# A fused two-layer encoder on one core: the decay product of the first GLA head is put directly behind the output gate's products, with its columns, and the PSUM banks are taken in another turn

## The chip, the cores and the metric

The kernel runs on one core of one Trainium2 chip. The core has a matrix engine (TensorE; PE in the profile, PEld for its weight loads), a vector engine (VectorE, DVE), a scalar engine (ScalarE, ACT), GpSimd (POOL) and a queue that issues transfers (SyncE, SP). Matrix products land in PSUM, of which this kernel uses eight banks of 128 partitions x 512 float32. The metric is device time in microseconds (us), the median of several executions. Before the change it is 2389.67 us (three executions, 2388.23 to 2390.68).

## What is computed

Two layers over a sequence of 1024 frames of width 1024: forgetting attention, a dense SwiGLU, gated linear attention (GLA), and again a SwiGLU, each normed, shifted, scaled and gated by a conditioning vector. The change lies in the GLA mixer:

```python
proj = h @ w_in
q, k, v, r, a_lr = jnp.split(proj, [...], axis=-1)
log_alpha = jax.nn.log_sigmoid((a_lr @ w_a2 + b_a)) / GLA_TAU
b = jnp.cumsum(log_alpha.reshape(B, N, CHUNK, GLA_HEADS, GLA_HK), axis=2)
q_in = q * jnp.exp(b)
k_in = k * jnp.exp(-b)
A = jnp.where(tril, jnp.einsum('bnthk,bnshk->bnhts', q_in, k_in), 0.0)
o_intra = jnp.einsum('bnhts,bnshv->bnthv', A, v)
k_dec = k * jnp.exp(b_last[:, :, None] - b)
kv = jnp.einsum('bnshk,bnshv->bnhkv', k_dec, v)
o = o_intra + o_inter            # o_inter = q_in times the state carried from chunk to chunk
o = rms_normed(o) * g_o * jax.nn.silu(r)
```

There are four heads, with 128 key columns and 256 value columns each. `a_lr` is 16 columns wide, and `(a_lr @ w_a2 + b_a)` is the decay.

## The kernel before

Every float32 matrix is held as a high and a low part, and a product is made as three (`mm3`, lines 289 to 292: high by high, high by low, low by high). A projection of 512 frames of one head (`proj`) runs over 8 slices of the width, so it is 24 products of 128x512 into one bank. Values go the other way round (`proj_tok`): 24 products for 128 frames.

The GLA part works head by head. Names below are those of the profile, with the lines of the kernel before.

- `gv`: values of the first head, eight tiles of 128 frames (`gv_first`). The weights of the values carry the 16 gate columns along, so a tile is 272 wide, and ScalarE copies these 16 columns to `aS`.
- `gr`: the output gate r, in halves of 512 frames (`r_proj`); ScalarE takes `silu` of a bank into `gs_s` (line 2061).
- `aps` and `aT`: four 128x16 blocks of gate columns are transposed into one bank (`a_body`) and split into high and low parts by ScalarE (line 1874), VectorE (1875) and ScalarE (1876).
- `z`: the decay product, one matrix product for 512 frames (`gate_z`). ScalarE takes the absolute value of it (`t_s`, line 1910), VectorE a clipped copy (`b_s`, line 1911).
- `gate_body`: exponential and logarithm on ScalarE (1918, 1919), a difference on VectorE (1920), two running sums (1923, TENSOR_TENSOR_SCAN), small columns `dec` (1927 to 1929), then exponentials on ScalarE into `ei_s` and `t_s` (1933, 1934).
- `gk`: keys, in two halves (`head_front`). VectorE reads a bank twice, times `ei_s` into `gy_s` and times `t_s` (1948, 1949); then the high and low parts `kih`, `kil`.
- `gqp`: queries, in two halves, read twice (1963) and split into `gq00`, `gq01`.
- `head_back`: transposes of the decayed keys (`kdt`, `kdh`, `kdl`), scores (`at`), masked (`atz`, line 1985) and split into `ahl`, states (`kv`, `Sf`, `S_t`) and outputs (`go`); the second half of the gate's columns (dv 1) is woven between these.

Beside it, VectorE works off steps of the second layer's conditioning vector (`ad_s`, lines 488 and 490), each of which waits for small transfers from the `ada_w` matrix, and the weights of what comes next are loaded and split: high part by ScalarE (line 227), low part by GpSimd in three pieces and VectorE in one (line 231).

What sets the order: each engine works through its own queue in order. The queues are made ahead of time by a scheduler that takes instructions as the program writes them and moves them by its own estimate of when each is ready; `tc.issue_after(x)` keeps what is written under it behind `x` on x's engine. PSUM banks are handed out in turn by rings. `pj` has banks b0, b1, b2, and its turns are, in the order of the program: `gr` first half, `z` first half, `gr` second half, `z` second half, `gk`, `gk`, `gqp`, `gqp`. The ring of the first head's values (`gvr`) has b0, b1, b2, b5, b6. So before the change the second half of `gr` has b2, which the last tile of values has just used, and the second `gk` has b2 as well; the second `gqp` has b1, the bank of the first `gk`.

## Time and profile before

| what | value |
|---|---|
| time of the runs, median | 2389.67 us |
| the profiled execution's own time | 2393.87 us |
| its span | 2392.2 us |
| TensorE busy | 2362.3 us, 99% of the span |
| VectorE busy | 1770.5 us, 74% |
| ScalarE busy | 1128.8 us, 47% |
| GpSimd busy | 1046.5 us, 44% |
| mean granted clock of TensorE | 0.991 |

A row of a timeline has the start in us from the span's start, the duration in us, the engine, the kernel's line, the operation, output <- inputs, the shape, how many instructions are merged, and in brackets how long the engine stood idle before it and what ended that. A row of the waits view has who waited for whom, the us in total, how many times, and the longest. Matrix products overlap in the pipeline: a 128x512 one lasts 0.39 us in these rows and the next starts about 0.23 us after it. Idle time of VectorE, ScalarE or GpSimd costs nothing as long as TensorE does not wait for them.

### The profile page before, as it was taken

The numbers are of one execution on the slowest core, as the hardware profiler recorded it, in microseconds if no ns is written. First come the engines' busy times: TensorE is split into PE (matmuls) and PEld (weight loads), VectorE is DVE, ScalarE is ACT, GpSimd is POOL, SyncE is SP. The second block draws the span as 40 slices with busy tenths as digits, with TensorE's granted clock in tenths as the row PEclk, the third lists the DMA queues.
The fourth block names the chain that finished last, engine by engine and source line by source line (L and its number), as shares of the span: only waits on it lengthen the run. The fifth ranks groups of instructions, "written<-read, shape, count | busy, mean of one in ns | idle before, by whom it ended". The sixth has DMA issues, their size and how long they took to land.

```text
span 2392.2 us, 35827 instructions
## 1 busy us (share of the span) xinstructions
PE 2362.3 (99%) x12312; PEld 2012.5 (84%) x12312; DVE 1770.5 (74%) x2985; ACT 1128.8 (47%) x2178; POOL 1046.5 (44%) x976
## 2 busy tenths in 40 slices
PE   8999999999999999999999999999999999999998
PEld 6988888888888888888888798898888888888888
DVE  6577787886698788875798566655687877765787
ACT  6656565675443333345325555453443333345326
POOL 1334444533445566643264321212345666643262
PEclk8999999999999999999999999999999999999999
DMA  8423333342435545457655233334424544457664
GB/s 259 142 80 113 104 119 93 119 133 89 150 109 174 178 165 168 166 203 258 228 188 166 82 105 90 99 112 132 150 91 154 179 148 161 154 180 255 230 205 147
DMA packets 336366, 363.47 MB, mean 152 GB/s; under 512 B 24924, under 2 KB 278008, under 8 KB 336184
## 3 DMA queue, kind: packets, MB, share of 16 engines
q1 hardware_dynamic: 336184, 361.18, 46.3%
q8 instruction: 97, 1.59, 0.3%
q14 instruction: 85, 0.70, 0.1%
HBM read 268.22 MB, written 92.86 MB: 151 GB/s over the span
## 4 chain that ended last, share of the span: by engine, by line
PE 82%; DVE 8%; DMA 4%; ACT 2%; issue 2%; POOL 1%; SPq 1%; DVEq 0%; POOLq 0%; ACTq 0%
PE p_b L290 15%; PE p_b L292 15%; PE p_b L291 15%; PE o_b L1224 2%; PE t_b L1210 2%; PE qk_b L290 1%; PE qk_b L291 1%; PE qk_b L292 1%; PE gr_b L290 1%; PE gr_b L291 1%; PE vps_b L292 1%; PE vps_b L290 1%; PE vps_b L291 1%; PE gr_b L292 1%; PE s_b L1178 1%
## 5 line engine op out<-in xcount | busy, mean ns | idle before, releaser
L175 DVE TENSOR_TENSOR o_s<-xv_s,o_s 128x512 fp32r<-128x512 f32 (+1 forms) x376 | 326.7, 874 | 67.7 <-ACT o_s L174 67.3
L174 ACT CAST o_s<-xv_s 128x512 fp32r<-128x512 f32 (+1 forms) x376 | 216.4, 587 | 304.3 <-PE p_b L292 244.5
L291 PE MATMUL p_b<-B,o_s 128*128 128x512 f32 x608 | 237.8, 391 | 0.0
L292 PE MATMUL p_b<-B,o_s 128*128 128x512 f32 x608 | 237.2, 391 | 0.0
L290 PE MATMUL p_b<-B,o_s 128*128 128x512 f32 x608 | 236.0, 391 | 0.0
L889 POOL TENSOR_TENSOR ex_s<-xv_s,xv_s 128x512 f32<-128x512 f32 (+1 forms) x64 | 88.5, 1382 | 286.7 <-DMA xv_s<-in_ffn_w_in_dram 113.6
L1190 POOL TENSOR_SCALAR lp_s<-lp_s,st 128x128 f32<-128x128 f32 (+7 forms) x128 | 97.9, 769 | 249.5 <-DVE st L1189 235.5
L290 PE MATMUL p_b<-T,o_s 128*128 128x512 f32 x480 | 186.7, 389 | 0.0
L291 PE MATMUL p_b<-T,o_s 128*128 128x512 f32 x480 | 186.7, 389 | 0.0
L292 PE MATMUL p_b<-T,o_s 128*128 128x512 f32 x480 | 181.2, 389 | 0.0
L292 PEld LDWEIGHTS p_b<-B,o_s 128*128 128x128 f32 x608 | 114.7, 189 | 24.0
L290 PEld LDWEIGHTS p_b<-B,o_s 128*128 128x128 f32 x608 | 114.7, 189 | 23.9
L291 PEld LDWEIGHTS p_b<-B,o_s 128*128 128x128 f32 x608 | 114.7, 189 | 23.7
L1188 ACT ACTIVATE lp_s<-lp_s,st 128x128 f32<-128x128 f32 (+7 forms) x128 | 99.3, 776 | 62.3 <-DVE st L1184 61.2
L891 POOL TENSOR_TENSOR xv_s<-ex_s,xv_s 128x512 f32<-128x512 f32 (+1 forms) x64 | 87.3, 1365 | 63.1 <-DVE o_s L175 60.8
L174 ACT CAST pt_s<-t_b 128x512 fp32r<-128x512 f32 (+1 forms) x160 | 79.8, 547 | 71.9 <-PE t_b L1210 71.3
L231 POOL TENSOR_TENSOR w_l_s<-w__s,w_h_s 128x256 fp32r<-128x256 f32 x90 | 69.6, 802 | 94.2 <-ACT w_h_s L227 61.8
L175 DVE TENSOR_TENSOR pt_s<-t_b,pt_s 128x512 fp32r<-128x512 f32 (+1 forms) x160 | 96.3, 630 | 15.9 <-ACT pt_s L174 15.4
L1572 DVE TENSOR_TENSOR ex_s<-ex_s,p_b 128x512 f32<-128x512 f32 x140 | 93.6, 681 | 18.6 <-PE p_b L292 18.5
L290 PEld LDWEIGHTS p_b<-T,o_s 128*128 128x128 f32 x480 | 90.1, 188 | 18.8
L291 PEld LDWEIGHTS p_b<-T,o_s 128*128 128x128 f32 x480 | 90.1, 188 | 18.7
L292 PEld LDWEIGHTS p_b<-T,o_s 128*128 128x128 f32 x480 | 90.1, 188 | 18.6
(1967 smaller groups left out, 7408.3 us busy)
## 6 DMA issues: line engine op xcount, KB each, us to landing
xv_s<-in_ffn_w_in_dram SPq DMA_DIRECT2D x176, 256.0 KB, 3.3
hid_B<-x SPq DMA_DIRECT2D x70, 512.0 KB, 2.8
ad_s<-in_ada_w_dram SPq DMA_DIRECT2D x384, 64.0 KB, 2.4
hid_T<-x SPq DMA_DIRECT2D x36, 512.0 KB, 2.8
xv_s<-in_ffn_w_out_dram SPq DMA_DIRECT2D x96, 192.0 KB, 5.1
ada_s<-in_ada_w_dram SPq DMA_DIRECT2D x96, 128.0 KB, 2.8
xv_s<-in_ffn_w_out_dram SPq DMA_DIRECT2D x40, 256.0 KB, 2.8
T2o<-hid_T SPq DMA_DIRECT2D x18, 512.0 KB, 9.7
```

The lines of the kernel that those rows point to most:

```text
L174: nc.scalar.copy(hi, src)
L175: nc.vector.tensor_sub(lo, src, hi.bitcast(F32))
L231: (nc.gpsimd if i < 3 else nc.vector).tensor_sub(lo[:, cs], rw[:, cs], hi[:, cs].bitcast(F32))
L290: nc.tensor.matmul(ps, ah, bh, start=start, stop=False)
L291: nc.tensor.matmul(ps, ah, bl, start=False, stop=False)
L292: nc.tensor.matmul(ps, al, bh, start=False, stop=stop)
L889: nc.gpsimd.tensor_add(s1, a21, a22)
L891: nc.gpsimd.tensor_sub(a11, s1, a11)
L1188: nc.scalar.activation(lp, lp, AF.Exp, bias=mcur, scale=-1.0, accum_out=st[:, qi, 2:3])
L1190: nc.gpsimd.tensor_scalar(lp, lp, st[:, qi, 3:4], 1.0, op0=ALU.mult, op1=ALU.mult)
L1210: nc.tensor.transpose(tp[:, i, :], lps[qi][:, psl(2 * b + jj)], ident)
L1572: nc.vector.tensor_add(d, d if src is None else dest(G, src), ps)
```

## The change

Four things are written differently, all for the first head.

1. After the ring of the values has been made, the turn of `pj` is moved on by one bank: `gr` takes b1 and b0, `z` b2 and b1, `gk` b2 and b0, `gqp` b1 and b2.
2. The second half of `gr` is begun (two slices, six products), then the gate columns of the second half are transposed behind those, then the other 18 products of `gr` behind the transposes, then `z` behind `gr`.
3. `gate_body` is put behind the last instruction of ScalarE, which is the absolute value of `z`.
4. The first head's `gk` products are put behind `z`.

```diff
@@ -1942,7 +1942,8 @@
             ps = pj([P, HALF], F32, f"gk{h}{hf}")
-            run(proj(ps, wk, h1, hf))
+            with ExitStack() if h else tc.issue_after(z_last):
+                run(proj(ps, wk, h1, hf))
             ada1(5.1)
@@ -2068,6 +2069,7 @@
     gvr = Ring(psp, list(pj.q) + list(opr.q))
+    pj.q.rotate(-1)
     aS = big.tile([P, 8, 16], F32, tag=kdr.q[0], name="aS")
@@ -2090,10 +2092,18 @@
     for t in range(4, 8):
         gv_first(t, wv)
-    while (0, 1) not in done:
+    for _ in range(2):
         next(rg)
-    a_body(1)
-    b16, t2, ei, dec = gate_body(0, gate_z(0, (1,), bt))
+    with tc.issue_after(last_of("P")):
+        a_body(1)
+    with tc.issue_after(last_of("P")):
+        while (0, 1) not in done:
+            next(rg)
+    with tc.issue_after(last_of("P")):
+        gate_z(0, (1,), bt)
+    z_last = last_of("P")
+    with tc.issue_after(last_of("A")):
+        b16, t2, ei, dec = gate_body(0, bt)
     gtile = {}
```

Since a scheduler makes the queues, the rows below show what became of them. TensorE's queue between the last tile of values and the second half of the keys, before:

```order
L292 MATMUL gv_b_8_13265<-wv_6h_s_81_12956,h1l_12670 128x272
L316 MATMUL aps_b_2_13327<-ident,aS 16x128 x3
L290 MATMUL gk_b_5_13378<-h1h_12655,w_h_s_85_12976 128x512
...
L316 MATMUL aps_b_2_13327<-ident,aS 16x128
...
L292 MATMUL gk_b_5_13378<-h1h_12669,w_l_s_86_12977 128x512
L290 MATMUL gr_b_3_13293<-h1h_12655,w_h_s_83_12966 128x512
...
L292 MATMUL gr_b_3_13293<-h1h_12669,w_l_s_84_12967 128x512
L1909 MATMUL z_b_4_13335<-aT,w2t 128x512
L290 MATMUL gk_b_6_13422<-h1h_12655,w_h_s_85_12976 128x512
```

and now:

```order
L292 MATMUL gv_b_8_13265<-wv_6h_s_81_12956,h1l_12670 128x272
L290 MATMUL gr_b_3_13293<-h1h_12655,w_h_s_83_12966 128x512
...
L316 MATMUL aps_b_2_13300<-ident,aS 16x128 x4
...
L292 MATMUL gr_b_3_13293<-h1h_12669,w_l_s_84_12967 128x512
L1909 MATMUL z_b_4_13335<-aT,w2t 128x512
L290 MATMUL gk_b_5_13378<-h1h_12655,w_h_s_85_12976 128x512
...
L292 MATMUL gk_b_5_13378<-h1h_12669,w_l_s_86_12977 128x512
L290 MATMUL gk_b_6_13422<-h1h_12655,w_h_s_85_12976 128x512
```

The first 24 products of the keys went from ahead of the gate's 24 to behind the decay product; the values of the eight tiles, which lay partly in each other before, now mostly stand tile after tile. The products of the queries (`gqp`) follow in both.

VectorE's queue around the gate columns and the decay (+ is the changed kernel, - the one before):

```order
 L231 TENSOR_TENSOR w_l_s_90_13369<-w__s_82_13366,w_h_s_89_13368 128x256
+L1875 TENSOR_TENSOR aT<-aps_b_2_13300,aT 16x512
 L490 TENSOR_SCALAR ad_s_12938<-ad_s_12939,c_164,ad_s_12938 128x256 x2
-L1875 TENSOR_TENSOR aT<-aps_b_2_13327,aT 16x512
 L490 TENSOR_SCALAR ad_s_12938<-ad_s_12938,c_164 128x256 x2
-L490 TENSOR_SCALAR ad_s_12938<-ad_s_12939,c_164,ad_s_12938 128x256 x2
 L231 TENSOR_TENSOR wv_0l_s_92_13465<-wv_0_s_83_13462,wv_0h_s_91_13464 128x256
 L1911 TENSOR_SCALAR b_0_s_1_13173<-z_b_4_13335,vec 128x512
+L490 TENSOR_SCALAR ad_s_12938<-ad_s_12939,c_164,ad_s_12938 128x256 x2
 L1920 TENSOR_TENSOR t_0_s_2_13174<-b_0_s_1_13173,t_0_s_2_13174 128x1024
```

The difference for `aT` moved ahead of two conditioning steps, and another two moved from ahead of `wv_0l` to between the clipped copy of z (1911) and the decay's difference (1920).

The last place is from the running sums to the masked scores. VectorE's queue at the masked scores, before:

```order
L1985 COPY_PREDICATED atz_s_12937<-tri,at_b_1_13582 128x512
L490 TENSOR_SCALAR ad_s_12938<-ad_s_12939,c_164,ad_s_12938 128x256
L1999 COPY Sf_13619<-kv_b_1_13615 128x256
L175 TENSOR_TENSOR kdl_s_2_13557<-kdt_b_4_13608,kdh_s_1_13556 128x512
L175 TENSOR_TENSOR ahl_s_1_13596<-atz_s_12937,ahl_s_1_13596 128x512
L175 TENSOR_TENSOR S_t<-Sf_13619,S_t 128x256
```

and now:

```order
L175 TENSOR_TENSOR gq01l_s_4_13475<-gy_s_12936,gq01h_s_3_13474 128x512
L1986 COPY_PREDICATED atz_s_12937<-tri,at_b_1_13582 128x512
L175 TENSOR_TENSOR ahl_s_1_13596<-atz_s_12937,ahl_s_1_13596 128x512
L2000 COPY Sf_13619<-kv_b_1_13615 128x256
L175 TENSOR_TENSOR kdl_s_2_13557<-kdt_b_4_13608,kdh_s_1_13556 128x512
```

`Sf` and the second `kdl` went from ahead of `ahl` to behind it. On ScalarE the two copies that make `wv_4h`, on which GpSimd's three pieces of `wv_4l` wait, stood between the decay's logarithm and its last exponentials; they now stand behind those and behind the first four exponentials for the queries (rows of the changed kernel):

```order
L1934 ACTIVATE t_0_s_2_13174<-b_0_s_1_13173,dec_13344 128x128
L174 COPY kih_s_1_13376<-gy_s_12936 128x512
L1953 ACTIVATE ei_s_3_13349<-b_0_s_1_13173,dec_13344 128x128 x4
L227 COPY wv_4h_s_93_13567<-wv_4_s_84_13565 128x512 x2
...
L1954 ACTIVATE b_0_s_1_13173<-b_0_s_1_13173 128x512 x2
```

The rows left out are `kih` and four exponentials of the second half.

## The prediction

> **What bounds the kernel now.** I read the page's head first, then the waits of the TensorE queue, then its timeline around the longest of them, and last the timelines of the engines that release it.

> ```profile
> span 2392.2 us, 35827 instructions
> PE 2362.3 (99%) x12312; PEld 2012.5 (84%) x12312; DVE 1770.5 (74%) x2985; ACT 1128.8 (47%) x2178; POOL 1046.5 (44%) x976
> PE gqp_b L290 <- DVE t_s L1949: 2.9, 1, 2.9
> PE gk_b L290 <- ACT gs_s L2061: 1.3, 1, 1.3
> ```

> TensorE is busy for 99% of the span. From 1296 us to the end its waits view has seven rows, and the two largest stand in the first head of the recurrence. So time is won here only where TensorE stands still or runs slowly, and what is won reaches the end unless it waits again. The stretch, from the last v product (gv) to the first transpose of k (kdt):

> ```profile
> 1332.73 0.29 PE L292 MATMUL gv_b<-wv_6h_s,h1l 128*128 128x272 f32 x1
> 1332.85 0.49 PE L316 MATMUL aps_b<-ident,aS 128*16 128x128 f32 x3
> 1333.10 0.48 PE L290 MATMUL gk_b<-h1h,w_h_s 128*128 128x512 f32 x1
> ...
> 1338.77 0.39 PE L290 MATMUL gr_b<-h1h,w_h_s 128*128 128x512 f32 x1
> ...
> 1344.20 0.39 PE L1909 MATMUL z_b<-aT,w2t 128*128 128x512 f32 x1
> 1345.91 0.50 PE L290 MATMUL gk_b<-h1h,w_h_s 128*128 128x512 f32 x1 [1.31 <-ACT gs_s L2061]
> ...
> 1351.48 0.39 PE L290 MATMUL gqp_b<-h1h,w_h_s 128*128 128x512 f32 x1
> ...
> 1356.69 0.39 PE L292 MATMUL gqp_b<-h1h,w_l_s 128*128 128x512 f32 x1
> ```

> ```profile
> 1359.96 0.50 PE L290 MATMUL gqp_b<-h1h,w_h_s 128*128 128x512 f32 x1 [2.88 <-DVE t_s L1949]
> 1360.29 0.39 PE L291 MATMUL gqp_b<-h1l,w_h_s 128*128 128x512 f32 x1
> ...
> 1361.23 0.63 PE L291 MATMUL gqp_b<-h1l,w_h_s 128*128 128x512 f32 x1
> 1361.66 0.63 PE L292 MATMUL gqp_b<-h1h,w_l_s 128*128 128x512 f32 x1
> ...
> 1367.16 0.60 PE L1975 MATMUL kdt_b<-ident,t_s 128*128 128x128 f32 x4
> ```

> Products are pipelined, so the cost of one is start to start: 24 of gr from 1338.77 to 1344.20 make 5.43 us, 0.226 each. The first wait costs 1345.91 - 1344.20 - 0.23 = 1.48 us, the second 1359.96 - 1356.69 - 0.23 = 3.04. Behind the second the products stand 0.43 apart (1361.23, 1361.66): the last 24 take 1367.16 - 1359.96 = 7.20 us where 24 should take 5.43, so 1.77 is lost to a halved clock. Together 6.3 us.

> The second wait is for the bank of the first k product, which is emptied by the two products with the decay factors (gy, t_s). These end a chain that the decay product z starts:

> ```profile
> 1344.22 1.14 ACT L227 CAST wv_0h_s<-wv_s 128x512 fp32r<-128x512 f32 x2 [4.29 <-PE gr_b L291]
> 1345.27 0.59 ACT L2061 ACTIVATE gs_s<-gr_b 128x512 f32<-128x512 f32 x1
> 1345.76 0.68 ACT L1910 ACTIVATE t_s<-z_b,vec 128x512 f32<-128x512 f32 x1
> 1351.21 1.23 DVE L1920 TENSOR_TENSOR t_s<-b_s,t_s 128x1024 f32<-128x1024 f32 x1 [4.00 <-ACT t_s L1919]
> 1352.47 3.27 DVE L1923 TENSOR_TENSOR_SCAN b_s<-ad_s,t_s 128x512 f32<-128x512 f32 x2
> 1358.62 0.69 DVE L1948 TENSOR_TENSOR gy_s<-gk_b,ei_s 128x512 f32<-128x512 f32 x1 [1.84 <-ACT ei_s L1933]
> 1359.22 0.68 DVE L1949 TENSOR_TENSOR t_s<-gk_b,t_s 128x512 f32<-128x512 f32 x1
> ```

> From z's start (1344.20) to the bank's release (1359.96) is 15.76 us. Only 48 products of 0.226 and the first wait cover it.

> **The change part by part.** *The turn of products.* The first 24 k products move from before gr's 24 to behind z. Nothing is added: 120 products at 0.226, four transposes of the gate columns (0.25 for three, 1332.85 to 1333.10, say 0.33) and z (0.23) are 27.7 us on both sides, and the trace took 1367.16 - 1332.85 = 34.3. The difference, 6.6, agrees with the 6.3 from the waits; I take 6.4. The new z starts at 1332.85 + 0.33 + 5.43 = 1338.6.

> *First wait.* gk's second half still takes the bank that gs_s reads. That read ended 1345.86 - 1344.20 = 1.66 us behind z, but 24 k products (5.4 us) now stand between. Cost nothing, covered with 3.8 us to spare.

> *Second wait.* The bank's release stays at most 15.76 behind z; TensorE now arrives after z and 72 products, 16.5 us. Covered by 0.7 us; if the chain were longer than that, each further us would be a us of wait. It should be shorter: the two scans took 3.27 beside POOL's low parts of wv_4, and the second head's took 2.33 without:

> ```profile
> 1352.19 4.07 POOL L231 TENSOR_TENSOR wv_4l_s<-wv_s,wv_4h_s 128x256 fp32r<-128x256 f32 x3 [4.98 <-ACT wv_4h_s L227]
> 1392.18 2.33 DVE L1923 TENSOR_TENSOR_SCAN b_s<-ad_s,t_s 128x512 f32<-128x512 f32 x2
> ```

> Those parts follow ScalarE's wv_4h copies, which now come behind four ei_s exponentials, so the scans run alone. With the wait goes the halved clock.

> *The gate columns.* Their chain (ScalarE, VectorE, ScalarE) must end before z. The last aS copy and the split ahead of it are where they were; aT's difference moves in front of two ad_s steps:

> ```profile
> 1335.62 0.95 DVE L231 TENSOR_TENSOR w_l_s<-w__s,w_h_s 128x256 fp32r<-128x256 f32 x1
> 1336.50 1.83 DVE L490 SCALAR_TENSOR_TENSOR ad_s<-ad_s,c,ad_s 128x256 f32<-128x256 f32 x2
> 1339.36 0.57 ACT L1876 CAST aT<-aps_b 16x512 fp32r<-16x512 f32 x1 [0.75 <-DVE aT L1875]
> 1342.74 1.00 DVE L490 SCALAR_TENSOR_TENSOR ad_s<-ad_s,c,ad_s 128x256 f32<-128x256 f32 x2 [1.59 <-DMA ad_s<-in_ada_w_dram]
> ```

> It can start at 1336.5 where those two started, takes about 0.7, and ScalarE's last copy 0.6: done by 1337.8, 0.8 before z. Nothing. The pair at 1342.74, which waits for its load, now stands between z's b_s and t_s L1920; behind it in the queue is the whole decay chain. L1920 is due at 1338.6 + 7.0 = 1345.6 and the pair ends at 1343.7 if its load lands as before. Nothing, with 1.9 to spare.

> *What is late next.* The masked scores (ahl) for the first output product (go). From the new z: 97 wide steps to kdt (22.0 us), then by the new order 30 gr products (6.8), 12 score products (1.4), two sets of transposes (0.8) and three of kv (0.4): go at z + 31.3. Before:

> ```profile
> 1368.87 1.16 DVE L175 TENSOR_TENSOR gq01l_s<-gy_s,gq01h_s 128x512 fp32r<-128x512 f32 x1
> 1372.03 0.68 DVE L175 TENSOR_TENSOR gq00l_s<-gy_s,gq00h_s 128x512 fp32r<-128x512 f32 x1
> 1375.12 0.62 ACT L174 CAST ahl_s<-atz_s 128x512 fp32r<-128x512 f32 x1
> 1375.97 0.68 DVE L175 TENSOR_TENSOR ahl_s<-atz_s,ahl_s 128x512 fp32r<-128x512 f32 x1
> 1379.80 0.28 PE L290 MATMUL go_b<-gvt_s,ahl_s 128*128 128x256 f32 x1
> ```

> go's first two products read ahl's high part, ready at 1375.74, z + 31.54, where go came at z + 35.6; its third reads the low part, ready at 1376.65, z + 32.45. With the old lags go would wait 0.25, and its third product, which the new order puts 0.7 us behind the first, another 0.2: 0.45. What shortens the lag: the scans give back about 1, and Sf's copy and the second kdl now stand behind ahl (another 1). What lengthens it: POOL's wv_4 parts now run beside the split of q (gq01l beside POOL took 1.16 where gq00l took 0.68, so 0.5 for each of two or three such operations), and two ad_s steps whose loads are issued early may wait for them. Bounds 0 (the gains count) and 2.0 (none does, and three operations are slowed); I take 0.9, the old lag and one slowed operation. So the saving is 6.4 - 0.9 = 5.5 us. SP's loads of weights keep their place until two sets of ad_s loads pass one weight load, which nobody here waits for.

> [...] The trace has the halved clock also behind a shorter gap, in the attention:

> ```profile
> 417.86 0.55 PE L1210 MATMUL t_b<-ident,lp_s 128*128 128x128 f32 x3 [1.84 <-POOL lp_s L1190]
> 419.17 0.63 PE L291 MATMUL qk_b<-h0l,w_h_s 128*128 128x512 f32 x1
> 419.60 0.63 PE L292 MATMUL qk_b<-h0h,w_l_s 128*128 128x512 f32 x1
> ```

> [...]

> **The sum.** The profiled execution took 2393.87 with a span of 2392.2, 4.2 above the median of the runs, 2389.67. Its span becomes about 2386.7. The saving is a difference within one place, so I carry it to the median: 2389.67 - 5.5 = 2384.2.

> **Rivals.**
> 1. *The masked scores take the wait's place.* go waits the upper bound, 2.0 us, and as behind the 1.84 us gap the clock halves, 1.77 more: the saving falls to 6.4 - 3.8 = 2.6, time 2387.1. For: VectorE is packed in that stretch. Against: Sf and kdl left its front.
> 2. *The slow products are not the wait's doing and stay.* Then 6.4 - 1.8 - 0.9 = 3.7 is saved, 2386.0. For: slow products stand without any gap elsewhere, behind 24 one-column products of the second feed-forward:

> ```profile
> 1733.89 3.04 PE L758 MATMUL sp_b<-ones,ss_s 128*128 128x1 f32 x24
> ...
> 1738.21 0.63 PE L290 MATMUL p_b<-B,o_s 128*128 128x512 f32 x1
> ```

> Against: the gap at 417.86, and that TensorE does next to nothing in both. [...]
> 3. *Given back later.* Loads that keep their own pace (ad_s, the next head's weights) become the bound and eat the gain: 0.5 saved, 2389.2. Against: no row of TensorE's waits view behind this stretch names a DMA.
> 4. *Slower.* The ad_s pair now ahead of L1920 waits for its load, and the decay chain with it. The spare is 1.9 at the pair and 0.7 at the bank, and 5.5 must be eaten: the load would have to land 8.1 us later than at 1342.74; at 10 us the time is 2391.6. Its loads stand on SP behind a weight load (wv_0) that waits for POOL's splits and may be issued a little later; nothing shows ten.

> That the order does not change is no rival: it stands above in z and the k products.

> **How the numbers follow.** Forecast 0.65 (its own range 2383.0 to 2385.7), rival 1 0.15, rival 2 0.08, rival 3 0.07, rival 4 0.05. The range 2382.4 to 2387.6 takes in both bounds of go's wait (0 gives 2383.3), 0.9 below for the scatter of the runs, and rivals 1 and 2. A measurement tells 0.2%, 4.8 us, from no change, so faster means under 2384.9: most of the forecast's chance, 0.54, and a little of rivals 1 and 2, 0.57 in all. Slower (over 2394.4) is a part of rival 4, 0.04. The rest, 0.39, is within.

> **What would show it.** In the new profile: z directly behind gr and about 5.6 us earlier than 1344.20; no wait of gk or gqp and no 0.63 us products in gqp; kdt near 1360.8; the scans near 2.3 us for two; a wait of go for ahl of under 2 us. Wrong: a wait of z for aT, of gqp for t_s, of L1920 behind ad_s, or a new stretch of 0.63 us products behind go.

## The result, and the profile after

The changed kernel takes 2383.41 us (median of eight executions, 2381.39 to 2385.01) where the kernel before took 2390.06 beside it: a ratio of 0.9969, 95% interval 0.9961 to 0.9977, or 5.5 to 9.3 us less. A second measurement (e8 below) gave 2385.11 against 2390.76, a ratio of 0.9972 (0.9963 to 0.9981). The medians alone lie 6.65 and 5.65 us apart. The predicted time was 2384.2.

| what | before | after |
|---|---|---|
| median of the runs | 2390.06 us | 2383.41 us |
| the profiled execution's own time | 2393.87 us | 2383.99 us |
| its span | 2392.2 us | 2382.3 us |
| last product of gv to first kdt | 34.43 us | 28.07 us |
| first kdt to the second kdt of the last head | 242.34 us | 243.25 us |

The head of the page of the changed kernel, and TensorE's first five rows of its waits view from 1296 us to the end (who waited for whom, us in total, times, the longest; two rows of 0.3 us follow):

```profile
span 2382.3 us, 35828 instructions
PE 2358.5 (99%) x12312; PEld 2011.4 (84%) x12312; DVE 1770.3 (74%) x2985; ACT 1129.7 (47%) x2178; POOL 1044.3 (44%) x976
```

```profile
PE ogt_b L2012 <- DVE on_t L2050: 0.9, 1, 0.9
PE ft_b L2165 <- ACT fz_s L2152: 0.8, 1, 0.8
PE go_b L290 <- ACT ahl_s L174: 0.6, 1, 0.6
PE kv_b L290 <- DVE Sf L2002: 0.4, 1, 0.4
PE p_b L292 <- DVE o_s L175: 0.4, 1, 0.4
```

The two rows that led this view before, gqp for t_s and gk for gs_s, are gone, and three small ones are new: go for ahl, kv for Sf, and p for o_s. The last stands far behind the stretch, at 2316.8 us, and the second profile of this kernel (e8) does not have it. TensorE's timeline over the stretch of the change:

```profile
1331.09 0.29 PE L292 MATMUL gv_b<-wv_6h_s,h1l 128*128 128x272 f32 x1
...
1332.61 0.60 PE L316 MATMUL aps_b<-ident,aS 128*16 128x128 f32 x4
...
1337.16 0.39 PE L1909 MATMUL z_b<-aT,w2t 128*128 128x512 f32 x1
1337.39 0.39 PE L290 MATMUL gk_b<-h1h,w_h_s 128*128 128x512 f32 x1
...
1353.71 0.39 PE L290 MATMUL gqp_b<-h1h,w_h_s 128*128 128x512 f32 x1
...
1358.92 0.39 PE L292 MATMUL gqp_b<-h1h,w_l_s 128*128 128x512 f32 x1
1359.16 0.60 PE L1976 MATMUL kdt_b<-ident,t_s 128*128 128x128 f32 x4
```

No row carries a bracket: TensorE waits for nothing between the values and kdt. The second half of gqp begins at 1353.71 and its 24 products take 1359.16 - 1353.71 = 5.45 us, at a granted clock of 1.00, where they took 7.20 at 0.76. The stretch from the last gv product to kdt is 28.07 us, 6.36 less than before (1367.16 - 1332.73 = 34.43). The chain that empties the bank, now (ScalarE, VectorE and, last, GpSimd):

```profile
1338.72 0.68 ACT L1910 ACTIVATE t_s<-z_b,vec 128x512 f32<-128x512 f32 x1
...
1344.17 1.23 DVE L1920 TENSOR_TENSOR t_s<-b_s,t_s 128x1024 f32<-128x1024 f32 x1 [1.57 <-ACT t_s L1919]
1345.44 2.34 DVE L1923 TENSOR_TENSOR_SCAN b_s<-ad_s,t_s 128x512 f32<-128x512 f32 x2
...
1350.91 0.68 DVE L1950 TENSOR_TENSOR t_s<-gk_b,t_s 128x512 f32<-128x512 f32 x1
...
1355.19 2.61 POOL L231 TENSOR_TENSOR wv_4l_s<-wv_s,wv_4h_s 128x256 fp32r<-128x256 f32 x3 [14.82 <-ACT wv_4h_s L227]
```

The bank is free at 1350.91 + 0.68 = 1351.59, 14.43 us behind z (15.76 before), and TensorE comes for it 1353.71 - 1337.16 = 16.55 behind z: 2.1 us to spare. The running sums take 2.34 us instead of 3.27. GpSimd's low parts of wv_4 now start 18.0 us behind z instead of 8.0 and no longer run beside them; e7 below, which brings them together again, has 3.25.

The two profiled spans differ by 9.9 us, more than the change made. 6.36 are the stretch; 0.91 of it is given back between kdt and the last head (243.25 - 242.34). The rest lies outside: 1.64 before the stretch (1332.73 - 1331.09) and 2.8 behind the last head. Both have rows in the view by windows (stretch in us: length, busy time and number of products, weight loads, VectorE, ScalarE, GpSimd, then the granted clock, the share of the DMA engines and GB/s), here of the kernel before and then of the changed one:

```profile
0.00:400.00 400.00, 387.91 (x2498) 343.32 (x2498) 284.74 (x681) 246.63 (x488) 160.54 (x235) 0.97 0.42 130
...
1720.00:1760.00 40.00, 40.00 (x184) 33.66 (x183) 28.66 (x45) 15.93 (x27) 9.16 (x7) 0.91 0.20 73
```

```profile
0.00:400.00 400.00, 390.37 (x2504) 346.51 (x2504) 284.57 (x682) 247.69 (x490) 161.17 (x237) 1.00 0.42 130
...
1720.00:1760.00 40.00, 40.00 (x195) 33.69 (x196) 31.81 (x49) 19.89 (x34) 11.40 (x8) 1.00 0.22 74
```

In both places the kernel before ran at a lower clock in its profiled execution (0.97 and 0.91 against 1.00), in work that the change does not touch. The 1.64 us is not the change's: in the second profile of the changed kernel (e8) the last gv product stands at 1332.68, where it stood before. By its own rows the change is worth 6.36 - 0.91 = 5.45 us.

### The profile page after: what moved, and what is told of

Same layout as the page of the kernel before. It is cut to its first block, busy times and chain, and to the rows that moved or that the text cites. A ratio compares the mean times of both kernels' runs of the same rounds, so it can differ in the third digit from the quotient of the medians.

```text
span 2382.3 us, 35828 instructions
## 1 busy us (share of the span) xinstructions
PE 2358.5 (99%) x12312; PEld 2011.4 (84%) x12312; DVE 1770.3 (74%) x2985; ACT 1129.7 (47%) x2178; POOL 1044.3 (44%) x976
## 3 DMA queue, kind: packets, MB, share of 16 engines
q8 instruction: 97, 1.59, 0.3%
## 4 chain that ended last, share of the span: by engine, by line
PE 84%; DVE 7%; DMA 3%; ACT 2%; issue 2%; POOL 1%; SPq 1%; DVEq 0%; POOLq 0%; ACTq 0%
PE p_b L290 15%; PE p_b L292 15%; PE p_b L291 15%; PE o_b L1224 2%; PE t_b L1210 2%; PE qk_b L290 1%; PE qk_b L291 1%; PE qk_b L292 1%; PE gr_b L290 1%; PE gr_b L291 1%; PE gr_b L292 1%; PE vps_b L290 1%; PE vps_b L291 1%; PE vps_b L292 1%; PE s_b L1178 1%
## 5 line engine op out<-in xcount | busy, mean ns | idle before, releaser
L175 DVE TENSOR_TENSOR o_s<-xv_s,o_s 128x512 fp32r<-128x512 f32 (+1 forms) x376 | 322.1, 862 | 67.5 <-ACT o_s L174 67.0
L174 ACT CAST o_s<-xv_s 128x512 fp32r<-128x512 f32 (+1 forms) x376 | 216.3, 587 | 304.3 <-PE p_b L292 241.5
L291 PE MATMUL p_b<-B,o_s 128*128 128x512 f32 x608 | 236.8, 389 | 0.0
L292 PE MATMUL p_b<-B,o_s 128*128 128x512 f32 x608 | 236.3, 389 | 0.0
L290 PE MATMUL p_b<-B,o_s 128*128 128x512 f32 x608 | 235.0, 390 | 0.0
L1190 POOL TENSOR_SCALAR lp_s<-lp_s,st 128x128 f32<-128x128 f32 (+7 forms) x128 | 97.7, 767 | 249.3 <-DVE st L1189 235.2
L290 PE MATMUL p_b<-T,o_s 128*128 128x512 f32 x480 | 186.7, 389 | 0.0
L291 PE MATMUL p_b<-T,o_s 128*128 128x512 f32 x480 | 186.7, 389 | 0.0
L292 PE MATMUL p_b<-T,o_s 128*128 128x512 f32 x480 | 181.2, 389 | 0.0
L292 PEld LDWEIGHTS p_b<-B,o_s 128*128 128x128 f32 x608 | 114.1, 188 | 23.8
L291 PEld LDWEIGHTS p_b<-B,o_s 128*128 128x128 f32 x608 | 114.1, 188 | 23.7
L290 PEld LDWEIGHTS p_b<-B,o_s 128*128 128x128 f32 x608 | 114.1, 188 | 23.5
L174 ACT CAST pt_s<-t_b 128x512 fp32r<-128x512 f32 (+1 forms) x160 | 79.8, 547 | 71.9 <-PE t_b L1210 71.3
L175 DVE TENSOR_TENSOR pt_s<-t_b,pt_s 128x512 fp32r<-128x512 f32 (+1 forms) x160 | 96.2, 629 | 15.7 <-ACT pt_s L174 15.2
L231 POOL TENSOR_TENSOR w_l_s<-w__s,w_h_s 128x256 fp32r<-128x256 f32 x90 | 69.6, 800 | 86.8 <-ACT w_h_s L227 53.4
L291 PEld LDWEIGHTS p_b<-T,o_s 128*128 128x128 f32 x480 | 90.1, 188 | 18.8
L290 PEld LDWEIGHTS p_b<-T,o_s 128*128 128x128 f32 x480 | 90.1, 188 | 18.7
L292 PEld LDWEIGHTS p_b<-T,o_s 128*128 128x128 f32 x480 | 90.1, 188 | 18.6
```

The source lines that it names most:

```text
L174: nc.scalar.copy(hi, src)
L175: nc.vector.tensor_sub(lo, src, hi.bitcast(F32))
L231: (nc.gpsimd if i < 3 else nc.vector).tensor_sub(lo[:, cs], rw[:, cs], hi[:, cs].bitcast(F32))
L290: nc.tensor.matmul(ps, ah, bh, start=start, stop=False)
L291: nc.tensor.matmul(ps, ah, bl, start=False, stop=False)
L292: nc.tensor.matmul(ps, al, bh, start=False, stop=stop)
```

## The experiments

Each is judged by two lengths in its profile: the stretch (last gv product to first kdt: 34.43 before, 28.07 changed) and what follows (first kdt to the last head's second kdt: 242.34 and 243.25). They do not contain the clock's changes in other places, which the total time does.

**e1, the turn of the banks alone**, in the kernel before:

```diff
     gvr = Ring(psp, list(pj.q) + list(opr.q))
+    pj.q.rotate(-1)
```

> The kernel before with the turn of the banks moved on by one and nothing else. In its queue of TensorE the decay product z now stands behind gr's 24, gk's first 24 and 9 products of gk's second half, so only 15 + 24 = 39 products lie between z and gqp's second half. Theory A (the gain is the cover: products between z and the bank's release): the first wait (gk for gs_s) is gone, but gqp's wait grows: release z + 14.6 (15.76 less the 1.1 us by which t_s no longer stands behind gs_s), cover 0.23 + 39 x 0.226 = 9.0, wait 5.6 us, and the halved clock behind it, 1.8. Together 7.4 against the 6.3 of the kernel before: 0 to 2.5 us slower than before. Theory B (the gain of the change comes from the banks): the waits shrink by themselves and this kernel is 3 us or more faster than before.

Measured: 2393.11 us against 2390.38, ratio 1.0009 (0.9999 to 1.0018), so no faster. The stretch is 1370.58 - 1334.49 = 36.09 us, 1.66 longer than before. TensorE and the running sums of this kernel:

```profile
1348.05 0.39 PE L1909 MATMUL z_b<-aT,w2t 128*128 128x512 f32 x1
...
1363.20 0.80 PE L290 MATMUL gqp_b<-h1h,w_h_s 128*128 128x512 f32 x1 [5.92 <-DVE t_s L1949]
...
1370.58 0.60 PE L1975 MATMUL kdt_b<-ident,t_s 128*128 128x128 f32 x4
```

```profile
1355.98 3.35 DVE L1923 TENSOR_TENSOR_SCAN b_s<-ad_s,t_s 128x512 f32<-128x512 f32 x2
```

Theory A holds: the first wait is gone and the second is 5.92 (5.6 expected). With a free bank for gk's second half, the scheduler had put nine products of it ahead of z as well. The turn alone gains nothing.

**e2, the order alone**: the changed kernel with the old turn.

```diff
-    pj.q.rotate(-1)
```

> The changed kernel with the old turn of the banks: gr's second half then takes the bank of the last tile of v. Theory A (cover): z stays directly behind gr and gqp does not wait, but gr's first product waits until the last tile has been copied out: in the kernel before 1335.16 - 1332.85 = 2.3 us lay between the last product of gv and the end of its last split. So a new wait of 1.5 to 2.6 us at gr, perhaps with a halved clock (up to 1.8): the stretch gains 6.4 - 2.3 - (0 to 1.8), that is 2.3 to 4.1 us against the kernel before, and 2.3 to 4.1 us are lost against the changed kernel. Theory B (the turn does not matter, the order does everything): no wait at gr, the time of the changed kernel within 1 us.

Measured: 2389.30 against 2390.38, ratio 0.9996 (0.9986 to 1.0006). The row of TensorE:

```profile
1334.59 0.50 PE L290 MATMUL gr_b<-h1h,w_h_s 128*128 128x512 f32 x1 [2.17 <-DVE gvt_s L175]
```

The expected wait is there, without slow products (those behind it stand 0.23 us apart, at a granted clock of 1.00), and gqp has none. The stretch is 1362.63 - 1332.13 = 30.50, so 3.93 less than before and 2.43 more than in the changed kernel; with what follows (243.29) 2.98 are left of the gain. The total shows 1.1, and its interval (3.3 less to 1.4 more) just holds 2.98. So order and turn belong together: the order removes the wait, the turn prevents the next.

**e3, the wait filled**: the kernel before, with 12 products into the two banks of opr, which are free there.

```diff
+            fill = None
+            if h == 0 and hf == 1:
+                with tc.issue_after(last_of("P")):
+                    for i in range(2):
+                        fp = opr([P, HALF], F32, f"fill{i}")
+                        for k in range(6):
+                            nc.tensor.matmul(fp, h1[k % 8].hi[:, 0:P], h1[k % 8].hi[:, cs], start=k == 0, stop=k == 5)
+                fill = last_of("P")
             ps = pj([P, HALF], F32, f"gqp{h}{hf}")
-            run(proj(ps, wq, h1, hf))
+            with tc.issue_after(fill) if fill is not None else ExitStack():
+                run(proj(ps, wq, h1, hf))
```

> The kernel before with 12 additional products of 128x512 (2.7 us, into two banks that are free there; nobody reads them) ahead of gqp's second half, where TensorE stood idle for 2.88 us. Theory A (the slow products follow from TensorE's standing idle): gqp's second half starts when it did, or up to 0.3 later, but its 24 products now stand 0.226 apart: about 1.8 us faster than the kernel before in the stretch from z to kdt (22.96 before, so 21.2), 2388.3 by the median. Theory B (rival 2 of the prediction, the slow products belong to the place and not to the wait): products of 0.63 us and 0.43 apart still stand behind the filler, z to kdt is 23.0 or more.

Measured: 2391.30 against 2390.38, ratio 1.0002 (0.9993 to 1.0012). In its timeline of TensorE:

```profile
1345.81 0.39 PE L1909 MATMUL z_b<-aT,w2t 128*128 128x512 f32 x1
...
1361.56 0.50 PE L290 MATMUL gqp_b<-h1h,w_h_s 128*128 128x512 f32 x1 [0.16 <-DVE t_s L1949]
...
1367.14 0.60 PE L1984 MATMUL kdt_b<-ident,t_s 128*128 128x128 f32 x4
```

gqp starts 15.75 us behind z, as before (15.76), but the 24 products take 5.58 instead of 7.20, and z to kdt is 21.33 (21.2 expected, 22.96 before). So the 1.77 us were the wait's doing and not the place's. The total is not shorter (2388.3 was expected). By the rows the 1.62 us are spent again behind the stretch: what follows takes 244.11 instead of 242.34, with new waits of go for S_t (0.5), kv for Sf (0.5) and kdt for kdl (0.3). I read it so that the products now come sooner than what they read, and that VectorE and ScalarE had lived on the time of the slow products; this was not tried apart.

**e4, the masked scores first**: the changed kernel, with the next head's decay chain put behind the second copy of ahl on ScalarE.

```diff
             ahl = intra(g)
+            if g:
+                ahl_hi.append(last_of("A"))
...
-            b16, t2, ei, dec = gate_body(h + 1)
+            with tc.issue_after(ahl_hi[-1]):
+                b16, t2, ei, dec = gate_body(h + 1)
```

> The changed kernel, with the exponential and the logarithm of the next head's decay put on ScalarE behind the copy of the masked scores (ahl) of the second half of each head. In the changed kernel that copy came at 1383.83 although its input was ready at 1378.10, and go waited 0.65 for it, then kv 0.41 for Sf behind the running sums. Theory A (these two waits were what the change gave back behind its stretch): the wait of go is gone, that of kv gone or below 0.5, nothing new waits: 0.6 to 1.1 us less than the changed kernel, 2382.5 by its median, 7 to 8 us less than before. Theory B (the copies only push the decay chain back): gk or gqp of the second head waits instead, as gqp did in the first, and the time is that of the changed kernel or worse.

It aims at these rows of the changed kernel (ScalarE, TensorE, VectorE):

```profile
1382.86 1.06 ACT L1919 ACTIVATE t_s<-t_s 128x1024 f32<-128x1024 f32 x1
1383.83 0.60 ACT L174 CAST ahl_s<-atz_s 128x512 fp32r<-128x512 f32 x1
```

```profile
1384.48 0.39 PE L290 MATMUL go_b<-gvt_s,ahl_s 128*128 128x256 f32 x1 [0.65 <-ACT ahl_s L174]
...
1388.86 0.38 PE L290 MATMUL kv_b<-gvt_s,kdh_s 128*128 128x256 f32 x1 [0.41 <-DVE Sf L2002]
```

```profile
1377.49 0.73 DVE L1986 COPY_PREDICATED atz_s<-tri,at_b 128x512 f32<-128x512 int32 x1
...
1386.10 2.33 DVE L1923 TENSOR_TENSOR_SCAN b_s<-ad_s,t_s 128x512 f32<-128x512 f32 x2
...
1388.35 0.45 DVE L2002 SCALAR_TENSOR_TENSOR Sf<-Sf,dec,kv_b 128x256 f32<-128x256 f32 x1
```

The scores are ready at 1378.1, but their copy stands behind the logarithm of the next head on ScalarE and comes at 1383.83; Sf stands behind the running sums. Measured: what follows kdt takes 242.50 instead of 243.25 us: go waits 0.2 in all, kv still 0.4. So 0.75 of the 0.91 given back is had again, and nothing new waits. In the total it is not to be seen (2382.5 was expected): 2385.43, ratio 0.9976 to the kernel before (0.9965 to 0.9986), within the interval of the changed kernel.

**e5, e6, e7, the cover in steps**: the changed kernel with 12, 18 and 24 of gk's first 24 products ahead of z. Each step of the loop in the diff makes three products, so the three kernels have `range(4)`, `range(6)` and `range(8)` there. (`gate_z` takes the bank as a new argument, and `head_front` leaves out what is already made; these lines are not shown.)

```diff
-    with tc.issue_after(last_of("P")):
-        gate_z(0, (1,), bt)
+    zps = pj([P, HALF], F32, "z01")
+    wk0 = feed.next()
+    gk0 = pj([P, HALF], F32, "gk00")
+    gk0g = proj(gk0, wk0, h1, 0)
+    with tc.issue_after(last_of("P")):
+        for _ in range(4):
+            next(gk0g)
+    with tc.issue_after(last_of("P")):
+        gate_z(0, (1,), bt, zps)
     z_last = last_of("P")
+    with tc.issue_after(z_last):
+        run(gk0g)
```

> The changed kernel with 12 of gk's first 24 products put back ahead of z, so that 60 instead of 72 products lie between z and gqp's second half. Theory A (only the cover counts: the bank is released 14.43 us behind z, TensorE arrives 0.23 + 0.226 a product behind it): gqp waits 14.43 - 13.8 = 0.6 us, the stretch from the last gv product to kdt is 28.07 + 0.6 = 28.7, no product of gqp is slow. Theory B (something else than the cover holds gqp, as the weights wv_4 or the steps of ad_s): no wait, or one above 1.5.

> As the one with 12 products ahead of z, but with 18, so that 54 lie between z and gqp's second half. Theory A (cover): gqp waits 14.43 - 12.45 = 2.0 us. On the clock, theory C (a gap's length decides: 1.84 us halved it, 1.31 us did not): the products behind the wait are slow and the stretch is 28.07 + 2.0 + 1.7 = 31.8. Theory D (stretches of 3.41 us on a grid of their own decide: where the products stream less than about 0.35 of what such a stretch can hold, the next one is at half clock; a gap of 2.17 us that lay across two of them did nothing): a gap of 2.0 us leaves 0.41 at the least, the products stay at 0.226, the stretch is 30.1.

> As the ones with 12 and 18 products ahead of z, but with all 24 of gk's first half, as before the change; the turn of the banks and the rest are the changed kernel's. ScalarE's wv_4h copies stand between the logarithm and the exponentials again. Theory A (cover): 48 products and z cover 11.1 us, gqp waits 3.3 us if the running sums run alone (2.34 us for two) and up to 4.7 if GpSimd's low parts of wv_4 slow them again (3.27); the stretch is 31.4 to 32.8, and 1.8 more with the halved clock, which both C (gap over 1.8) and D (a gap of 3.3 leaves under 0.35 in one grid stretch in most places of the grid) expect here. Theory B (the gain is not the cover but the order of gr and gk or the turn of the banks): a wait below 2 us.

| products of gk ahead of z | gqp's wait | bank free behind z (by gqp's start where it waits) | two running sums | stretch |
|---|---|---|---|---|
| 0 (changed kernel) | none | 14.43 us | 2.34 us | 28.07 us |
| 12 (e5) | none | 13.32 | 2.34 | 28.06 |
| 18 (e6) | 0.74 us | 13.38 | 2.34 | 29.14 |
| 24 (e7) | 3.36 us | 14.63 | 3.25 | 33.36 |

```profile
1345.09 0.69 ACT L1910 ACTIVATE t_s<-z_b,vec 128x512 f32<-128x512 f32 x1 [2.85 <-PE z_b L1909]
```

```profile
1358.04 0.50 PE L290 MATMUL gqp_b<-h1h,w_h_s 128*128 128x512 f32 x1 [0.74 <-DVE t_s L1950]
```

```profile
1349.20 3.25 DVE L1923 TENSOR_TENSOR_SCAN b_s<-ad_s,t_s 128x512 f32<-128x512 f32 x2
```

(The first two rows are e6, whose z starts at 1344.66, the third is e7.) The wait grows as products leave the cover, but theory A's 0.6 and 2.0 us came out as none and 0.74. By the letter, e5's "no wait" is theory B's outcome. But nothing else held gqp: the lag that theory A took for a constant is none. With work between gr and z, ScalarE has wv_0h and gs_s behind it when z comes, and starts 0.43 us behind z instead of 1.56. So 13.3 to 13.4 is the chain's own length. TensorE is done with the product ahead of gqp's second half at z + 14.00, 12.64 and 11.27 in the three kernels, 1.36 and 1.37 less for six products fewer each time. 13.32, 13.38 and 14.63 less these give no wait, 0.74 and 3.36. e7's chain is longer because the sums are slowed by 0.9 us and the first of the small columns behind them by 0.36 (0.53 instead of 0.17): wv_4h stands ahead of the exponentials again, and GpSimd's low parts of wv_4 run from 1348.49 to 1352.98. Its gqp runs at half clock: granted 0.50 from 1358.10 to 1361.52, and 7.22 us for the 24 products.

e5 was not as quiet as the table says. What follows its kdt took 245.02 us, 1.77 more than in the changed kernel. These rows of TensorE and VectorE carry it:

```profile
1367.03 0.66 PE L1976 MATMUL kdt_b<-ident,t_s 128*128 128x128 f32 x4 [2.24 <-DVE kdl_s L175]
```

```profile
1362.33 0.48 DVE L490 SCALAR_TENSOR_TENSOR ad_s<-ad_s,c 128x256 f32<-128x256 f32 x1 [1.26 <-DMA ad_s<-in_ada_w_dram]
1362.73 1.23 DVE L175 TENSOR_TENSOR gq01l_s<-gy_s,gq01h_s 128x512 fp32r<-128x512 f32 x1
1363.88 0.95 DVE L490 SCALAR_TENSOR_TENSOR ad_s<-ad_s,c 128x256 f32<-128x256 f32 x1
```

A step of ad_s waits 1.26 us for its load with VectorE's queue behind it, two operations behind it take 1.23 and 0.95 (the same split took 0.68 at 1367.88, the step ahead of it 0.48), and kdl, which frees the bank of kdt, comes 2.24 us too late. Each of the three kernels was executed once: 2385.94, 2388.07 and 2389.83 us, and 2394.15 for the kernel before beside them. Whether the late load comes again in other executions is therefore not known. e6 did not tell theories C and D apart, as its gap was only 0.74; they are settled by other rows, in the last section.

**e8, the changed kernel again, and e9, one tile of squares**: e9 is e4 with the squares of three norms added up on VectorE first.

```diff
-    LATE1 = 7
+    LATE1 = 8
...
-                if h_ == 1 and m in SUM_AT:
+                if h_ == 1 and m in SUM_AT and LATE1 != 8:
```

> The changed kernel once more, beside the next one on the same chip. Theory A (its saving is 6.4 in the stretch less about 0.9 that is given back at go and kv): 5.5 us under the kernel before, a ratio of 0.9977. Theory B (the larger difference of the medians, 6.7 to 7.4 us, is the change's own): 0.9970.

> The version with ahl first, and beside it the sums of squares of three norms (the two of the feed-forwards' second halves and that of the mixer's second half) added up by VectorE to one tile before they go to TensorE: 4 one-column products instead of 16 at each place; the sums are taken in another order, nothing is left out. Theory D (few streamed columns in a grid stretch of 3.41 us halve the clock in the next, gap or not): without the block of one-column products of 2.8 us (302 columns in 9 us of work before and behind it) the halved stretches near 1302 and 1736 us are gone, 1.7 us each, and 8 products fewer at 0.24 each in a block give 1.9 us more per place; against it two more additions of 0.7 us in each chain. If those are covered by other products: 5 to 8 us less than the changed kernel. Theory E (the additions are on the path): sp or rb waits 1.4 to 2.1 us at each of three places, a gap that may halve the clock itself, and the time is that of the changed kernel within 2 us.

e8: 2385.11 against 2390.76, ratio 0.9972 (0.9963 to 0.9981); its stretch is 28.07 and what follows 243.31, so 5.39 us by the rows, as in the first profile. Both theories lie in the interval. e9: 2392.25, ratio 1.0003 (0.9994 to 1.0012), 7 us over the changed kernel. The mechanism of theory E holds, but its time (that of the changed kernel within 2 us) does not; from e9's waits view:

```profile
PE sp_b L758 <- DVE ss_s L771: 6.2, 2, 3.2
PE sp_b L758 <- DVE se_s L771: 1.4, 1, 1.4
```

The additions are on the path at all three places, with waits of 3.0, 1.4 and 3.2 us (1.4 to 2.1 expected), and the clock halves behind these waits as it did behind the one-column products: behind the waits of 3.0 and 3.2 us products of 512 columns stand 0.43 us apart (from 659.97 and from 1736.14), behind that of 1.4 us products of 272 columns 0.23 apart (from 1307.46), where 0.125 was usual (1298.46 to 1302.86). So e9 does not tell what those products cost by themselves.

## Why the prediction was right

**The waits and their cover.** Both waits are gone as worked out. z came 6.07 us behind the last gv product (1337.16 - 1331.09) where it had come 11.47 behind it: 5.4 earlier, 5.6 predicted. kdt came 22.0 behind z, as predicted. With the 1.63 us by which the whole stretch started earlier added (its first work began at 1331.22, not 1332.85), kdt stands at 1360.8, the number of the prediction. The stretch gained 6.36, the sum said 6.4. This part was right in its mechanism and in its size.

**The second wait's margin** was 0.7 us or more, and it is 2.1, as the bank is free 1.33 us earlier behind z. The running sums gave 0.93 of it, as expected from the second head's row, and e7, which takes wv_4h back between the logarithm and the exponentials, lengthened them to 3.25 again. e5 and e6 show that the cover sets the wait.

**The gate columns** were done at 1335.53 + 0.58 = 1336.11, 1.05 us before z (0.8 predicted):

```profile
1335.53 0.58 ACT L1876 CAST aT<-aps_b 16x512 fp32r<-16x512 f32 x1 [1.70 <-DVE aT L1875]
```

**The ad_s pair** ahead of L1920 did not hold the chain: L1920 waited for the logarithm (1.57 <- t_s L1919), at z + 7.0. Rival 4 named a mechanism that exists: in e5 an ad_s load held VectorE for 1.26 us, and it is a part of the 2.24 us for which kdt waited there.

**What is late next** is the term that was mis-sized, or rather misplaced: "I take 0.9, the old lag and one slowed operation". go waited 0 at that place. These rows of the changed kernel carry it:

```profile
1367.84 0.62 ACT L174 CAST ahl_s<-atz_s 128x512 fp32r<-128x512 f32 x1 [2.55 <-DVE atz_s L1986]
```

```profile
1368.62 0.28 PE L290 MATMUL go_b<-gvt_s,ahl_s 128*128 128x256 f32 x1
```

ahl's high part is ready at 1368.46, z + 31.30, and go comes at z + 31.46: it fits by 0.16 us. The lower bound of 0 was the right end, since no operation of that chain was slowed. But the time was given back 16 us later, in the second half of the same head, 0.65 at go and 0.41 at kv, less the 0.2 that go had waited before: some 0.85, and 0.91 by the lengths. The prediction ended its look at the first go. So 6.4 - 0.9 = 5.5 was right in its sum, but the 0.9 was luck: it stands in the sum for a wait that did not come, and another wait that the prediction did not look for has the same size. e4 shows where most of it comes from, ScalarE's order in the next head's chain: with that order changed, 0.75 of the 0.91 is had again.

**The rivals.** Rival 1 did not happen: no slow products stand behind go (granted clock 1.00 from 1368.60 to 1602). Rival 2 (the slow products stay) is refuted twice, by the changed kernel's gqp at 0.227 us a product and by e3, where the wait was filled and the slowness went. Rival 3 did not happen: behind the stretch no wait for a DMA is among TensorE's rows.

**The carrying to the median** is the one step that is not settled. The rows give 5.45 and 5.39 us in two profiles; the measured differences are 7.4 (5.5 to 9.3) and 6.7 (4.5 to 8.8) by the ratios, 6.65 and 5.65 by the medians. The first interval has 5.5 at its edge, so more may have been saved than the rows of the change show. The forecast does not hang on this: with 5.45 off the 2390.06 measured beside it, the time would be 2384.6. The halved clock near 1736 us is a candidate for the difference: in the profile of the kernel before it is 0.50 from 1736.15 to 1742.98, in that of the changed kernel 1.00 from 1720 to 1760, and in e9 products stand 0.43 us apart from 1736.14 to 1738.70. What stands behind the second kdt of the last head takes 782.7 us in the kernel before, 779.3 to 779.9 in the two profiles of the changed kernel and 779.3 and 780.0 in e1 and e6, and 781.0 to 782.1 in e2 to e5 and e7. From these lengths I take it that 3.41 us at half clock stand there in e2 to e5 and e7, and none in e1, e6 and e8 (an estimate, with 1.7 us lost in 3.41). e1 has the order of products closest to the kernel before and is among the short ones, and e4 and e5 are among the longer ones though they are close to the changed kernel; that speaks for chance. Whether the change makes that block run at full clock as a rule was not tried, and the rest of the difference stays open.

**Part 3 of the change** (gate_body behind the absolute value): what it is worth by itself is not shown by any run.

## What to carry to other kernels

Where one engine waits for a chain that one of its own products starts, count the products between that start and the place where the result is needed, and move the start, not the waiter: each product brought behind it moved the moment of need by its own 0.226 us (six moved it by 1.36 to 1.37 us in e5 to e7), until the chain was covered. Free the place for it in the ring of buffers in the same step, or the wait comes back at the neighbour (e2), and a scheduler may use a freed buffer to make the order worse (e1). Look for the return of a gain past the first consumer: here, and again in e3, TensorE arrived sooner at the next stages and waited there for the side engines.

## What the runs showed of the clock

| kernel | from, us | length, us |
|---|---|---|
| before | 418.61 | 3.41 |
| before | 1302.66 | 3.41 |
| before | 1360.69 | 3.41 |
| before | 1736.15 | 6.83 |
| changed | 417.70 | 3.41 |
| changed | 1301.75 | 3.41 |

In the kernel before they begin 884.05, 58.03 and 375.47 us apart, which is 259, 17 and 110 times 3.413, and in the changed kernel 884.05 again. So I divide each of the two executions into stretches of 3.413 us that begin where these do. Three neighbouring ones in the kernel before, around gqp's wait (length, TensorE's busy time, number of its products, granted clock, DMA share, GB/s):

```profile
1353.86:1357.27 3.41, 3.22 (x15) 1.00 0.00 0
1357.27:1360.68 3.41, 0.72 (x3) 1.00 0.55 154
1360.68:1364.10 3.42, 3.42 (x10) 0.50 0.00 0
```

Three products fell into the middle one, and the next ran at 0.50. Behind the one-column products, where TensorE is busy all the time:

```profile
1732.74:1736.15 3.41, 3.41 (x28) 1.00 0.47 185
1736.15:1739.57 3.42, 3.42 (x12) 0.50 0.00 0
```

And e2 around its 2.17 us wait at gr, in pieces of the same length:

```profile
1329.88:1333.30 3.42, 2.54 (x21) 1.00 0.02 2
1333.30:1336.71 3.41, 2.12 (x11) 1.00 0.56 162
1336.71:1340.12 3.41, 3.41 (x16) 1.00 0.51 127
```

The wait lies across two of them, and the clock stayed at 1.00. It stayed so behind e5's 2.24 us (1368.71 to 1372.12, behind a piece with 1.68 us of work), though 1.84 us had halved it at 417.86 in the kernel before, and 1.93 us at 417.05 in the changed one. So theory C falls. For theory D I counted, for each stretch at full clock in the two profiles, the columns that products stream in it, against those of 128x512 products 0.226 us apart. The shares are 0.12, 0.18, 0.25 and 0.34 in the four of the kernel before that a halved one follows, and 0.23 and 0.23 in the two of the changed kernel. The other 1321 have 0.47 or more, and none of them has a halved one behind it. Theory D holds for these two executions; where between 0.34 and 0.47 its limit lies, they do not show (in e7 a piece with six products, about 0.4, had a halved one behind it).

At gqp's wait the halved clock cost 1.77 us; 1.7, half of 3.41, is the estimate for a stretch full of work. Near 1302 us, behind the one-column products there, 3.41 us ran at 0.50 in both profiles, near 1736 us 6.83 in the kernel before and none in the changed one. With 0.35 as the limit, as theory D has it, a gap of 3.04 us as at gqp before leaves one stretch with 0.35 of its work or less in about six of ten places where the stretches can begin (an estimate from the shares above: one stretch must hold 2.2 us of the gap). So the 1.77 us of this case were lost in the profiled execution, but some executions of the kernel before need not have lost them.
